# One more product in seven quarter products, with the Z projection's units between them, and moved copies and sums, in a hybrid decoder layer

## The chip, the cores and the metric

One core of a Trainium2 chip runs the whole layer. The metric is device microseconds (us) of one execution. TensorE (PE) multiplies, VectorE (DVE) and ScalarE (ACT) work on the results, the queues of SyncE (SP), ACT and GpSimd (POOL) issue transfers.

## The reference, cut to what matters

The layer has 512 tokens of width 1024. From `h`, the normalised input, it makes three token mixers, merges them under gates and projects the sum. The change touches the third mixer, the gates and the end:

```python
u, v, z = jnp.split(h @ w_in_c, 3, axis=-1)
u = jax.nn.gelu(u)
v = layernorm(jax.nn.gelu(v), ln_g, ln_b)
sp = jnp.einsum('gij,bnjgc->bnigc', wm, vr) + b_s.T[:, :, None]    # vr: v by 128-token chunks
y_c = u * sp.reshape(Bsz, S, MIX_W) * jax.nn.silu(z)
...
g_i = jax.nn.sigmoid(h @ w_in[:, G_OFF + i * D_MODEL:G_OFF + (i + 1) * D_MODEL])
merged = sum over i of g_i * (ys[i] @ w_br[i])
out = rmsnorm(merged @ w_out, g_post)
return x + gate[:, None] * out
```

The v projection, the z and u projections and each gate are products of 512 x 1024 by 1024 x 1024; all are float32.

## The kernel before, in words

**How a product is done.** A float32 operand is split in two fp32r parts, a rounded one (`split`, L71, ACT) and the rest (L72, DVE). Three of the four cross products are taken, so one 128 x 128 x 512 step is three matmuls: L102, L104, L106 in `chan` (channels on the output partitions) and L856, L858, L860 in `passes` (tokens on the output partitions). A pass of 12 matmuls makes 128 tokens by 512 columns over half of the 1024 inputs.

**The chain.** From about 507 us on, everything is a list of units run by `Chain.run`. A unit has a loader, which issues its transfers and gives the steps that split its weights, and a generator, which yields after each matmul. While unit n multiplies, the split steps of unit n+1 are put after its matmuls 1, 2, 3 and so on, extra steps (`also`) at places that L817 sets from the unit's length n, and evictions wait in `later` for a number of matmuls (LAG is 5). These places set only the order of the instructions in each engine's stream. PE, DVE, ACT, SP and POOL each run their stream in that order, and start an instruction as soon as its operands and buffers allow.

**Order of the units.** Gate 0 (4 units of 48 matmuls, `plain`), branch 0 (4 of 48, `add_branch`), gate 1 (7 of 24, `Seven`), branch 1 (4 of 48), v (4 of 48, `plain`), then for each of four column groups a z unit and a u unit (48 each), gate 2 (7 of 24, `Seven`), branch 2 (4 of 48), and the output projection: `out_first(0)`, `out_first(4)` (48 each) and `out_second` (96).

**Seven.** This class makes a product from seven quarter products in place of eight. `p1`, `p2`, `p5`, `p6`, `p7`, `p3`, `p4` run in this order, 24 matmuls each. `p6` adds to the bank that `p1` left in PSUM, `p7` and `p4` add on to the same bank, so a copy of its state (`us`, L927, ACT) must be taken before `p7` writes it. Sums and differences of weight quarters are built in the three tiles `big`: by ACT with factor -1 and a transfer of POOL's queue that accumulates (`minus`, L967 and L968), by such a transfer alone (`plus`, L972), or on DVE (L986). `load` (L962) brings two quarters in, during `p7` and `p3` of the Seven before it (`after`). Results are put together by DVE (`add`, L908) and handed to the evict function. The sums of h that the class needs (`h_sums`) are made once, during gate 0.

**Buffers.** PSUM holds four banks `g`, two `x` (the Sevens' `p1`, `p6`, `p7`, `p4`) and two `t`. `t` serves the transposes of the merged rows (`turn_m`, L1073, released by a split), the spatial product of u (L1130), `gate_sum`, and in `piece` the throw-away output of the Square (L1301). SBUF has five tiles `th`. Each evicted v or u goes through `gelu`, a Square and a Tanh on ACT with DVE steps between them; v ends in `v_evict` and, after the last, `v_norm`. A z unit (`u_z2`) leaves its silu in a `th` tile that the u unit after it uses up; the u unit's result lies in a tile `yc`.

**The end.** During branch 2 the eight steps of `gate(j)` (L1278, L1280) accumulate one fourth of the output gate from transfers of SP's queue. `gate_sum(j)` (L1285, two matmuls into `t`, then L1287 and L1288 on DVE) finishes it. The four calls stand in `out_first(0)` after its last row block, and in `out_first(4)` after the first three. Between these two units ACT's queue issues the loads of x (L1360). `piece(t, e)` takes a finished half of 128 output rows: Square on ACT (L1301), product with the gate on DVE (L1302), and for the second half the root, the sum with x (L1309) and the store.

Of the kernel before, what the change touches and what calls it, by code (L numbers as in the profile page):

```python
# [15 lines left out]
S = 512  # L16
D = 1024
# [20 lines left out]
def hybrid_block(ctx, tc, x, c, g_pre, g_post, w_ada, b_ada, w_in, conv_w, conv_b, pos_ck, w_ck1, w_ck2,  # L38
# [729 lines left out]
    class Chain:  # L768
# [37 lines left out]
        def run(self, upto=None):  # L806
            while self.n < (len(self.units) if upto is None else upto):
                if self.ready is None:
                    self.prepare()
                (w, steps), (_, gen, n, also) = self.ready, self.units[self.n]  # L810
                for f in steps[self.given:]:
                    f()
                self.n += 1
                self.ready, self.given = None, 0
                self.prepare()
                todo = [(1 + k, f) for k, f in enumerate(self.ready[1] if self.ready else [])]
                todo += [(6 + (n - 8) * k // max(1, len(also)), f) for k, f in enumerate(also)]  # L817
                todo.sort(key=lambda x: x[0])
                at = 0
                for _ in gen(w):  # L820
                    at += 1
                    while todo and todo[0][0] <= at:
                        todo.pop(0)[1]()
                    self.tick()
                for _, f in todo:
                    f()
                self.given = len(self.ready[1]) if self.ready else 0
# [64 lines left out]
    class Seven:  # L892


        def __init__(self, src, evict):
            self.src = src
            self.evict = evict
            n = len(mats)
            self.a, self.b, self.c = [big[i] for i in ((0, 1, 2) if n % 2 == 0 else (1, 0, 2))]
            self.after = None  # L900
            if mats:
                mats[-1].after = self
            mats.append(self)
            self.loaded = [False, False]
            ps, us, ys, zs, bs5 = {}, {}, {}, {}, {}

            def add(lag, d, b, t, e):
                chain2.later((lag, lambda: tt(d, b, d, op=OP.add)), (lag + 8, lambda: evict(d, t, e)))  # L908

            def p1(w):  # L910
                for i in range(2):
                    ps[i] = bank("x")
                    yield from passes(ps[i], A11(i), w, True, True)
                    zs[i] = th_tile()
                    chain2.later((LAG, lambda i=i: act(zs[i], ps[i], AF.Copy)))

            def p2(w):
                for i in range(2):
                    z = bank()
                    yield from passes(z, A12(i), w, True, True)  # L920
                    add(18, zs[i], z, i, 0)

            def p6(w):
                for i in range(2):
                    yield from passes(ps[i], S2(i), w, False, True)
                    us[i] = th_tile()
                    chain2.later((LAG, lambda i=i: act(us[i], ps[i], AF.Copy)))  # L927

            def p5(w):
                for i in range(2):  # L930
                    bs5[i] = bank()
                    yield from passes(bs5[i], S1(i), w, True, True)
                    ys[i] = th_tile()
                    chain2.later((LAG, lambda i=i: act(ys[i], bs5[i], AF.Copy)))

            def p3(w):
                for i in range(2):
                    yield from passes(bs5[i], S4(i), w, False, True)
                    add(LAG, us[i], bs5[i], i, 1)

            def p7(w):
                for i in range(2):
                    yield from passes(ps[i], S3(i), w, False, True)
                    add(LAG, ys[i], ps[i], 2 + i, 1)

            def p4(w):
                for i in range(2):
                    yield from passes(ps[i], A22(i), w, False, True)
                    chain2.later((LAG, lambda i=i: evict(ps[i], 2 + i, 0)))

            for load, gen in ((self.l1, p1), (self.l2, p2), (self.l5, p5), (self.l6, p6), (self.l7, p7), (self.l3, p3),
                              (self.l4, p4)):
                chain2.add(load, gen, 24)

        def at(self, i, j, k=0, n=4):
            return self.src[512 * i + 128 * k:512 * i + 128 * (k + n), 512 * j:512 * j + 512].rearrange("(k p) c -> p k c", p=128)
# [80 lines left out]
    def add_branch(i):  # L1037
        src = w_br[0, i]
        bs = {}

        def merge(t, e):
            d = ths.pop((t, e))
            stt(d, d, 1.0, bs[t], op0=OP.add, op1=OP.mult)  # L1043
            if i == 0:
                merged[t, e] = d
                return
            tt(merged[t, e], merged[t, e], d, op=OP.add)
            if i == 2:
                turns.append((t, e))

        def gen(e, k0):
            def f(w):
                for t in range(NB):
                    if k0 == 0:
                        bs[t] = bank()
                    yield from passes(bs[t], y_side(t, k0), w, k0 == 0, k0 == 4)
                    if k0 == 4:
                        chain2.later((LAG, lambda t=t: merge(t, e)))
                    if len(turns) > 2:
                        turn_m(*turns.pop(0))  # L1060
            return f

        for e in range(2):
            for k0 in (0, 4):
                chain2.add(lambda e=e, k0=k0: block(src, k0, 512 * e), gen(e, k0), 48)
# [2 lines left out]

    def turn_m(t, e):

        t_ = t_tile()
        for k in range(4):
            nc.tensor.transpose(t_[:, k * 128:k * 128 + 128], merged[t, e][:, k * 128:k * 128 + 128], ident)  # L1073
        ks = slice(4 * e, 4 * e + 4)
        split(mt[0][:, ks, t * 128:t * 128 + 128], mt[1][:, ks, t * 128:t * 128 + 128],
              t_.rearrange("p (k c) -> p k c", c=128))


    def gelu(src, last):

        th = th_tile()
        act(th, src, AF.Square, scale=GELU_A ** 0.5)
        chain2.later((3, lambda: stt(th, th, 1.0, src, op0=OP.add, op1=OP.mult)),
                     (6, lambda: act(th, th, AF.Tanh, scale=GELU_S)),
# [20 lines left out]
        for t in range(NB):  # L1105
            ts(vg[:, t, :], vg[:, t, :], mv[:, t, 0:1], lr[:, 1, t:t + 1], op0=OP.subtract, op1=OP.mult)

    zs2 = {}

    def u_z2(w):  # L1110
        for e in range(2):
            ps = bank()
            yield from chan(ps, w, e, hh, hl)
            th = zs2[e] = th_tile()
            chain2.later((LAG, lambda th=th, ps=ps: act(th, ps, AF.Tanh, scale=0.5)),
                         (LAG + 3, lambda th=th, ps=ps: stt(th, th, 1.0, ps, op0=OP.add, op1=OP.mult)))

    def u_u2(j):
        def f(w):
            for e in range(2):  # L1120
                ps = bank()
                yield from chan(ps, w, e, hh, hl)

                def last(th, e=e, ps=ps, z=zs2[e]):
                    stt(th, th, 1.0, ps, op0=OP.add, op1=OP.mult)
                    tt(z, z, th, op=OP.mult)
                    g = 2 * j + e
                    t_ = t_tile()
                    for n in range(NB):
                        mm(t_[:, n * 128:(n + 1) * 128], vg[:, n, g * 128:(g + 1) * 128], wst[:, g, :], start=True, stop=True)  # L1130
                    yc[g] = keep.tile([128, S], F, name=f"qy{g}")
                    chain2.later((6, lambda: stt(yc[g].rearrange("p (n i) -> p n i", n=NB), t_.rearrange("p (n i) -> p n i", n=NB),
                                                 lgh[:, g:g + 1], bi[:, g, None, :].to_broadcast([128, NB, 128]),
                                                 op0=OP.mult, op1=OP.add)),
                                 (7, lambda: tt(yc[g], yc[g], z, op=OP.mult)))
                chain2.later((LAG, lambda ps=ps, last=last: gelu(ps, last)))
        return f

# [16 lines left out]
    def chan_load(col):  # L1155
# [1 line left out]
            w, steps = load_w(w_in, col)  # L1157
            return w, [lambda s=s: split(*s) for s in steps]
        return f

    yc = {}

    def h_side(t, k0):
        return lambda k: tuple(a[:, k0 + k, t * 128:t * 128 + 128] for a in (hh, hl))
# [25 lines left out]
    n1 = len(chain2.units)  # L1190
    add_branch(1)
    n2 = len(chain2.units)
    plain(w_in[:, C_V:C_V + D], v_evict)
    n3 = len(chain2.units)
    for j in range(KT // 2):
        chain2.add(chan_load(C_Z + 256 * j), u_z2, 48)
        chain2.add(chan_load(C_U + 256 * j), u_u2(j), 48)
    gates_of(2)
    n4 = len(chain2.units)
# [45 lines left out]
    w_spatial()  # L1245
    chain2.run(n2 + 3)
    b_spatial()
    chain2.run(n3 + 8)
    chain2.flush()
    cst.close()  # L1250
    yst = ExitStack()
# [46 lines left out]

    def piece(t, e):
        cs = slice(512 * e, 512 * e + 512)  # L1300
        act(t_tile(), bs[t], AF.Square, accum_out=s2[:, t, e:e + 1])  # L1301
        tt(ots[t][:, cs], bs[t], gpb[:, cs], op=OP.mult)  # L1302
        if e == 0:
            ts(s2[:, t, 3:4], s2[:, t, 0:1], 1.0 / D, 16.0 * EPS, op0=OP.mult, op1=OP.add)
# [4 lines left out]
            stt(ots[t][:, cs], ots[t][:, cs], s2[:, t, 4:5], xts[t][:, cs], op0=OP.mult, op1=OP.add)  # L1309
            nc.sync.dma_start(out[t * 128:(t + 1) * 128, cs], ots[t][:, cs])  # L1310

    gates_left = list(range(4))

    def out_first(k0):
        def f(w):
            for t in range(NB):
# [2 lines left out]
                yield from passes(bs[t], m_side(t, k0), w, k0 == 0, k0 == 4)  # L1319
                if turns:  # L1320
                    turn_m(*turns.pop(0))
                elif k0 == 0:
                    gate_sum(gates_left.pop(0))
                if k0 == 4:
                    if gates_left:
                        gate_sum(gates_left.pop(0))
                    chain2.later((LAG, lambda t=t: piece(t, 0)))
        return f

# [63 lines left out]
```

## Time and profile before

| | us |
|---|---|
| three runs | 968.57, 969.81, 970.11; median 969.81 |
| the profiled execution | 971.98 |
| its span, first to last instruction | 970.3 |
| mean granted clock of TensorE, share of full speed | 0.992 |
| PE, DVE, ACT busy | 929.1, 686.7, 473.7 |
| slowest lines of the waits of PE after 480 us | 4.7, 2.6, 1.2 |

Start times in rows are us from the span's start. A PE row's duration covers a pipelined matmul, so successive rows overlap; what a matmul costs the stream is the distance between two starts. A wait in brackets is the idle time before the instruction and what ended it.

### The profile page before, as it was taken

How to read it: one execution, taken by the hardware profiler on the slowest of the kernel's cores; microseconds unless marked ns; L12 is line 12 of the kernel's file. 1: busy time of each engine (PE TensorE's matmuls, PEld its weight loads, DVE VectorE, ACT ScalarE, POOL GpSimd, SP SyncE). 2: the span in 40 equal slices, each digit the busy share in tenths (PEclk: the TensorE clock that was granted, in tenths of full speed). 3: DMA queues.
4: the chain of work that ended last, by engine and by line, in shares of the span. 5: the costliest groups of instructions: out<-in, count | busy, mean ns of one | idle time of the engine just before them, and what ended most of it. 6: DMA issues, size and time to landing. Idle time of an engine off the chain costs nothing.

```text
span 970.3 us, 13192 instructions
## 1 busy us (share of the span) xinstructions
PE 929.1 (96%) x4561; PEld 776.6 (80%) x4561; DVE 686.7 (71%) x1673; ACT 473.7 (49%) x1010; POOL 34.3 (4%) x58
## 2 busy tenths in 40 slices
PE   2999999999999999999999999999999999999986
PEld 1789978878887888888888888788878888787765
DVE  5867488998889889989848435645467555657836
ACT  5546366665556666665534415622333334642411
POOL 2010000000000000000010001200000001100000
PEclk9999999999999999999999999999999999999988
DMA  9937021131211213112242424744333323545622
GB/s 288 321 97 221 1 83 49 45 87 44 82 49 48 83 45 87 45 55 76 68 151 87 131 87 88 173 130 124 105 97 109 87 87 67 107 146 177 192 93 88
DMA packets 87337, 101.93 MB, mean 105 GB/s; under 512 B 6841, under 2 KB 67365, under 8 KB 87269
## 3 DMA queue, kind: packets, MB, share of 16 engines
q1 hardware_dynamic: 80484, 86.22, 29.8%
q0 software_dynamic: 4736, 10.66, 5.2%
q10 hardware_dynamic: 2048, 4.19, 1.2%
q8 instruction: 36, 0.59, 0.3%
q14 instruction: 33, 0.26, 0.1%
HBM read 98.96 MB, written 2.10 MB: 104 GB/s over the span
## 4 chain that ended last, share of the span: by engine, by line
PE 69%; issue 14%; DMA 7%; DVE 5%; ACT 2%; POOL 1%; SPq 1%; DVEq 0%; ACTq 0%; POOLq 0%
PE g L102 11%; PE g L104 11%; PE g L106 11%; PE g L858 5%; PE g L860 5%; PE g L856 5%; PE o L697 4%; PE t L686 4%; PE s L664 3%; DMA wa<-in_w_ada_dram 2%; DMA raw<-in_w_out_dram 2%; PE f L273 2%; DMA big<-in_w_in_dram 1%; PE s L471 1%; DVE wl L72 1%
## 5 line engine op out<-in xcount | busy, mean ns | idle before, releaser
L106 PE MATMUL g<-hh,wl 128*128 128x512 f32 x528 | 211.7, 401 | 0.0
L102 PE MATMUL g<-hh,wh 128*128 128x512 f32 x528 | 211.4, 400 | 0.0
L104 PE MATMUL g<-hl,wh 128*128 128x512 f32 x528 | 211.3, 400 | 0.0
L72 DVE TENSOR_TENSOR wl<-raw,wh 128x512 fp32r<-128x512 f32 x228 | 145.4, 686 | 88.8 <-ACT wh L71 81.1
L71 ACT ACTIVATE wh<-raw 128x512 fp32r<-128x512 f32 x228 | 128.1, 622 | 157.6 <-PE g L860 76.3
L104 PEld LDWEIGHTS g<-hl,wh 128*128 128x128 f32 x528 | 99.4, 188 | 16.8
L102 PEld LDWEIGHTS g<-hh,wh 128*128 128x128 f32 x528 | 99.4, 188 | 16.8
L106 PEld LDWEIGHTS g<-hh,wl 128*128 128x128 f32 x528 | 99.4, 188 | 16.6
L676 ACT ACTIVATE p<-p,mx 128x384 f32<-128x384 f32 (+3 forms) x128 | 71.1, 557 | 39.7 <-DVE mx L674 38.9
L856 PE MATMUL g<-wh,y 128*128 128x512 f32 x192 | 75.2, 392 | 0.4 <-DVE qy L1043 0.4
L860 PE MATMUL g<-wh,y 128*128 128x512 f32 x192 | 74.8, 389 | 0.0
L858 PE MATMUL g<-wl,y 128*128 128x512 f32 x192 | 74.7, 389 | 0.0
L71 ACT ACTIVATE ph<-t 128x512 fp32r<-128x512 f32 (+3 forms) x128 | 55.5, 434 | 38.6 <-PE t L686 37.1
L674 DVE CUSTOM_DVE_ANT_0 p<-s,D 128x384 f32<-128x384 f32 (+3 forms) x128 | 60.5, 484 | 18.1 <-PE s L664 17.4
L856 PE MATMUL g<-wh,hh 128*128 128x512 f32 x176 | 71.2, 405 | 0.0
L858 PE MATMUL g<-wl,hh 128*128 128x512 f32 x176 | 69.5, 395 | 0.0
L860 PE MATMUL g<-wh,hl 128*128 128x512 f32 x176 | 69.5, 395 | 0.0
L72 DVE TENSOR_TENSOR pl<-t,ph 128x512 fp32r<-128x512 f32 (+3 forms) x128 | 61.9, 485 | 5.5 <-ACT ph L71 4.4
L686 PE MATMUL t<-ident,p 128*128 128x128 f32 x320 | 56.9, 276 | 1.4 <-DVE pl L72 1.4
L679 DVE TENSOR_SCALAR p<-p,mx,gates 128x384 f32<-128x384 f32 (+3 forms) x128 | 55.5, 442 | 1.7
L72 DVE TENSOR_TENSOR wl<-big,wh 128x1024 fp32r<-128x1024 f32 x24 | 28.7, 1223 | 32.4 <-ACT wh L71 32.4
L664 PE MATMUL s<-kst,qst 128*128 128x288 f32 (+2 forms) x192 | 50.1, 342 | 1.2 <-DVE mx L674 1.2
(296 smaller groups left out, 1646.6 us busy)
## 6 DMA issues: line engine op xcount, KB each, us to landing
raw<-in_w_in_dram SPq DMA_DIRECT2D x180, 256.0 KB, 3.4
raw<-in_w_br_dram SPq DMA_DIRECT2D x48, 256.0 KB, 3.4
big<-in_w_in_dram POOLq DMA_DIRECT2D x20, 512.0 KB, 6.1
wa<-in_w_ada_dram SPq DMA_DIRECT2D x32, 256.0 KB, 6.3
rawg<-in_w_ada_dram SPq DMA_DIRECT2D x16, 256.0 KB, 3.7
raw<-in_w_out_dram SPq DMA_DIRECT2D x16, 256.0 KB, 3.5
rawf<-in_w_in_dram SPq DMA_DIRECT2D x6, 512.0 KB, 6.6
xt<-in_x_dram SPq DMA_DIRECT2D x4, 512.0 KB, 5.2
```

The lines of the kernel that those rows point to most:

```text
L71: act(dst_h, src, AF.Copy)
L72: tt(dst_l, src, dst_h, op=OP.subtract)
L102: mm(ps, w[0][:, k, cs], rh[:, k, :], start=(k == 0), stop=False)
L104: mm(ps, w[0][:, k, cs], rl[:, k, :], start=False, stop=False)
L106: mm(ps, w[1][:, k, cs], rh[:, k, :], start=False, stop=(k == KT - 1))
L664: mm(s_[:, :o + n], q[:, i * 128:(i + 1) * 128], ks[:, z, b, 32 - o:32 + n], start=(z == 0), stop=(z == 1))
L674: nc.vector.tensor_tensor_reduce(out=p, in0=s_, in1=D0[:, S - n:], scale=-slopes[h], scalar=LIM, op0=OP.add, op1=OP.min, accum_out=mx[:, 0 ...
L676: act(p, p, AF.Exp, bias=mx[:, 0, i:i + 1], scale=-1.0, accum_out=mx[:, 1, i:i + 1])
L686: nc.tensor.transpose(t_[:, (i - j) * 128:(i - j + 1) * 128], ps[i][:, j * 128:(j + 1) * 128], ident)
L856: mm(ps, h_, part(w[0], k), start=f, stop=False, skip_group_check=True)
L858: mm(ps, h_, part(w[1], k), start=False, stop=False, skip_group_check=True)
L860: mm(ps, l_, part(w[0], k), start=False, stop=e, skip_group_check=True)
```

## The change

- v becomes a `Seven`. The four z units are put between its products: one after `p2`, one after `p6`, one after `p3`, one after `p4`. The u units then follow one another.
- z is kept in the tile `yc` of its group from the z unit on; the spatial result goes through a `th` tile and is multiplied into it. `gelu` gets three tiles of its own.
- In all three Sevens, `us` is copied at once after its pass in place of 5 matmuls later, and `ys` 9 matmuls later in place of 5.
- The extra steps of a unit (`also`) start a third into it and not at matmul 6. This moves the splits of branch outputs, the sums of h and the steps of `gate`.
- `gate_sum(0)`, `(1)`, `(2)` move to branch 2, after the third row block of its second, third and fourth unit; `gate_sum(3)` takes the place that `gate_sum(0)` had.
- Every second `turn_m` uses a bank `x` in place of `t`; the Square of `piece` writes to a `th` tile in place of `t`.

```diff
-                todo += [(6 + (n - 8) * k // max(1, len(also)), f) for k, f in enumerate(also)]
+                todo += [(n // 3 + (2 * n // 3 - 4) * k // max(1, len(also)), f) for k, f in enumerate(also)]
...
-                    chain2.later((LAG, lambda i=i: act(us[i], ps[i], AF.Copy)))
+                    act(us[i], ps[i], AF.Copy)
...
-                    chain2.later((LAG, lambda i=i: act(ys[i], bs5[i], AF.Copy)))
+                    chain2.later((9, lambda i=i: act(ys[i], bs5[i], AF.Copy)))
...
+            for n, (load, gen) in enumerate(((self.l1, p1), (self.l2, p2), (self.l5, p5), (self.l6, p6), (self.l7, p7),
+                                             (self.l3, p3), (self.l4, p4))):
                 chain2.add(load, gen, 24)
+                for u in between.get(n, ()):
+                    chain2.add(*u)
...
                     if len(turns) > 2:
                         turn_m(*turns.pop(0))
+                    if i == 2 and t == 2 and (e or k0):
+                        gate_sum(2 * e + k0 // 4 - 1)
...
-        t_ = t_tile()
+        t_ = bank("x") if (t + e) % 2 else t_tile()
...
-        th = th_tile()
+        th = cp_.tile([128, S], F, name="ge", bufs=3)
...
-    plain(w_in[:, C_V:C_V + D], v_evict)
+    zu = [(chan_load(C_Z + 256 * j), u_z2(j), 48) for j in range(KT // 2)]
+    Seven(w_in[:, C_V:C_V + D], v_evict, {1: zu[:1], 3: zu[1:2], 5: zu[2:3], 6: zu[3:]})
     n3 = len(chain2.units)
     for j in range(KT // 2):
-        chain2.add(chan_load(C_Z + 256 * j), u_z2, 48)
         chain2.add(chan_load(C_U + 256 * j), u_u2(j), 48)
...
-        act(t_tile(), bs[t], AF.Square, accum_out=s2[:, t, e:e + 1])
+        act(th_tile(), bs[t], AF.Square, accum_out=s2[:, t, e:e + 1])
...
                 if turns:
                     turn_m(*turns.pop(0))
-                elif k0 == 0:
-                    gate_sum(gates_left.pop(0))
+                if k0 == 0 and t == 3:
+                    gate_sum(3)
                 if k0 == 4:
-                    if gates_left:
-                        gate_sum(gates_left.pop(0))
                     chain2.later((LAG, lambda t=t: piece(t, 0)))
```

## Rows read from the trace of the kernel before

**Rows 1.** The page: busy time, share and instructions of each engine.
```profile
PE 929.1 (96%) x4561; PEld 776.6 (80%) x4561; DVE 686.7 (71%) x1673; ACT 473.7 (49%) x1010; POOL 34.3 (4%) x58
```

**Rows 2.** Waits of PE, 480 to 972 us: total, times, longest (us).
```profile
PE t L1285 <- ACT t L1301: 4.7, 1, 4.7
PE x L856 <- ACT th L927: 2.6, 2, 1.9
PE t L1073 <- DVE hl L72: 1.2, 1, 1.2
```

**Rows 3.** PE's timeline in gate 1: start, us, engine, line, operation [idle before].
```profile
599.67 0.39 PE L860 MATMUL g<-wh,hl 128*128 128x512 f32 x1
...
615.31 0.39 PE L860 MATMUL x<-wh,hs1l 128*128 128x512 f32 x1
616.38 0.50 PE L856 MATMUL x<-wh,hs2h 128*128 128x512 f32 x1 [0.68 <-ACT th L927]
```

**Rows 4.** PE's timeline in gate 2, from p6 to p7.
```profile
838.44 0.39 PE L860 MATMUL x<-wh,hs1l 128*128 128x512 f32 x1
840.73 0.50 PE L856 MATMUL x<-wh,hs2h 128*128 128x512 f32 x1 [1.90 <-ACT th L927]
...
844.94 0.39 PE L860 MATMUL x<-wh,hs2l 128*128 128x512 f32 x1
```

**Rows 5.** Windows of 10 us: busy time PE, PEld, DVE, ACT, POOL, PEclk, DMA share, GB/s.
```profile
840.00:850.00 10.00, 9.27 (x34) 7.48 (x35) 6.05 (x8) 5.98 (x10) 0.00 (x0) 0.83 0.18 34
```

**Rows 6.** ACT's timeline in gate 2, same stretch.
```profile
837.09 1.06 ACT L71 ACTIVATE wh<-big 128x1024 fp32r<-128x1024 f32 x1 [0.67 <-DMA big<-in_w_in_dram]
...
839.05 1.14 ACT L71 ACTIVATE y<-qy 128x512 fp32r<-128x512 f32 x2
840.09 0.58 ACT L927 ACTIVATE th<-x 128x512 f32<-128x512 f32 x1
```

**Rows 7.** PE's timeline, output projection.
```profile
916.47 0.66 PE L1073 MATMUL t<-ident,ya 128*128 128x128 f32 x4
...
919.98 0.58 PE L856 MATMUL g<-wh,hh 128*128 128x512 f32 x1
...
925.85 0.39 PE L860 MATMUL g<-wh,hl 128*128 128x512 f32 x1
930.92 1.22 PE L1285 MATMUL t<-acc,ones 128*128 128x256 f32 x2 [4.69 <-ACT t L1301]
...
940.21 0.39 PE L856 MATMUL g<-y,hh 128*128 128x512 f32 x1
```

**Rows 8.** ACT's timeline and its queue (ACTq), output projection.
```profile
918.44 1.56 ACTq L1360 DMA_DIRECT2D big<-in_x_dram  x3
...
927.71 0.63 ACT L71 ACTIVATE y<-raw 128x512 fp32r<-128x512 f32 x1 [1.31 <-DMA raw<-in_w_out_dram]
929.64 0.63 ACT L71 ACTIVATE y<-raw 128x512 fp32r<-128x512 f32 x1 [1.29 <-DMA raw<-in_w_out_dram]
930.17 0.58 ACT L1301 ACTIVATE t<-g 128x512 f32<-128x512 f32 x1
```

**Rows 9.** DVE's timeline, end of branch 2 and output projection.
```profile
915.11 0.69 DVE L1047 TENSOR_TENSOR ya<-ya,qy 128x512 f32<-128x512 f32 x1
...
930.91 0.42 DVE L1287 TENSOR_TENSOR gpb<-t,gpb 128x256 f32<-128x256 f32 x1
```

**Rows 10.** Windows from the start of v to the last u (columns as rows 5).
```profile
676.40:816.80 140.40, 140.40 (x653) 116.77 (x652) 83.90 (x145) 51.59 (x89) 3.96 (x3) 1.00 0.35 97
```

**Rows 11.** Groups by line and shape, 480 to 975 us: busy us, mean ns, idle before.
```profile
L72 DVE TENSOR_TENSOR wl<-raw,wh 128x512 fp32r<-128x512 f32 x132 | 83.7, 687 | 77.0 <-ACT wh L71 76.6
L72 DVE TENSOR_TENSOR wl<-big,wh 128x1024 fp32r<-128x1024 f32 x24 | 28.7, 1223 | 32.4 <-ACT wh L71 32.4
L908 DVE TENSOR_TENSOR th<-g,th 128x512 f32<-128x512 f32 x8 | 5.4, 684 | 0.0
```

**Rows 12.** The page: DMA issues, KB each, median us from issue to landing.
```profile
big<-in_w_in_dram POOLq DMA_DIRECT2D x20, 512.0 KB, 6.1
```

More of the change, by code (lines that the diff above doesn't have):

```diff
@@ L892, in hybrid_block, with __init__ @@
     class Seven:
-        def __init__(self, src, evict):
+        def __init__(self, src, evict, between={}):
             self.src = src
@@ L949, in p4 @@
                     chain2.later((LAG, lambda i=i: evict(ps[i], 2 + i, 0)))
-            for load, gen in ((self.l1, p1), (self.l2, p2), (self.l5, p5), (self.l6, p6), (self.l7, p7), (self.l3, p3),
-                              (self.l4, p4)):
+            for n, (load, gen) in enumerate(((self.l1, p1), (self.l2, p2), (self.l5, p5), (self.l6, p6), (self.l7, p7),
+                                             (self.l3, p3), (self.l4, p4))):
                 chain2.add(load, gen, 24)
+                for u in between.get(n, ()):
+                    chain2.add(*u)
         def at(self, i, j, k=0, n=4):
@@ L1106, in v_norm, with u_z2, f @@
             ts(vg[:, t, :], vg[:, t, :], mv[:, t, 0:1], lr[:, 1, t:t + 1], op0=OP.subtract, op1=OP.mult)
[L1108 to L1116, printed above, removed]
+    yc = {}
+    def u_z2(j):
+        def f(w):
+            for e in range(2):
+                ps = bank()
+                yield from chan(ps, w, e, hh, hl)
+                z = yc[2 * j + e] = keep.tile([128, S], F, name=f"qy{2 * j + e}")
+                chain2.later((LAG, lambda z=z, ps=ps: act(z, ps, AF.Tanh, scale=0.5)),
+                             (LAG + 3, lambda z=z, ps=ps: stt(z, z, 1.0, ps, op0=OP.add, op1=OP.mult)))
+        return f
     def u_u2(j):
@@ L1122, in f, with last @@
                 yield from chan(ps, w, e, hh, hl)
-                def last(th, e=e, ps=ps, z=zs2[e]):
+                def last(th, ps=ps, g=2 * j + e):
+                    z = yc[g]
                     stt(th, th, 1.0, ps, op0=OP.add, op1=OP.mult)
                     tt(z, z, th, op=OP.mult)
-                    g = 2 * j + e
                     t_ = t_tile()
@@ L1130, in last @@
                         mm(t_[:, n * 128:(n + 1) * 128], vg[:, n, g * 128:(g + 1) * 128], wst[:, g, :], start=True, stop=True)
-                    yc[g] = keep.tile([128, S], F, name=f"qy{g}")
-                    chain2.later((6, lambda: stt(yc[g].rearrange("p (n i) -> p n i", n=NB), t_.rearrange("p (n i) -> p n i", n=NB),
+                    d = th_tile()
+                    chain2.later((6, lambda: stt(d.rearrange("p (n i) -> p n i", n=NB), t_.rearrange("p (n i) -> p n i", n=NB),
                                                  lgh[:, g:g + 1], bi[:, g, None, :].to_broadcast([128, NB, 128]),
                                                  op0=OP.mult, op1=OP.add)),
-                                 (7, lambda: tt(yc[g], yc[g], z, op=OP.mult)))
+                                 (7, lambda: tt(z, z, d, op=OP.mult)))
                 chain2.later((LAG, lambda ps=ps, last=last: gelu(ps, last)))
@@ L1159, in chan_load @@
         return f
-    yc = {}
     def h_side(t, k0):
@@ L1247, in hybrid_block @@
     b_spatial()
-    chain2.run(n3 + 8)
+    chain2.run(n3 + 4)
     chain2.flush()
@@ L1310, in piece @@
             nc.sync.dma_start(out[t * 128:(t + 1) * 128, cs], ots[t][:, cs])
-    gates_left = list(range(4))
     def out_first(k0):
```

## The prediction

> **What bounds the kernel now.** I read the page's busy times first: PE is busy for 96% of the span, DVE for 71% [rows 1]. Next the waits of PE after 480 us, where all that changes lies: three lines, 8.5 us together, are nearly all it waits [rows 2]. So time can be won in two ways only, with fewer matmuls or with these waits. Then PE's timeline, for what one matmul costs. From 599.67 to 615.31 us, 69 starts follow each other without a wait: 15.64 / 69 = 0.2267 us each [rows 3]. The 0.39 us in each row is the length of a pipelined matmul and not its price.
>
> The waits cost more than their own length. Before `p7` of gate 1 the distance is 1.07 us in place of 0.23, so about 0.9 us are lost with the slower start behind it [rows 3]. Before `p7` of gate 2 it is 2.29 us, and from there to 844.94 us twelve matmuls take 6.50 us in place of 12 x 0.2267 = 2.72: 3.8 us lost, since the matmuls behind the wait run slower [rows 4]. The granted clock of that window is 0.83 [rows 5], so a part of it was at 1.2 GHz and not at 2.4. Both waits end with the copy of `us`. In gate 2, ACT is late because a weight split waits for an accumulated transfer until 837.09 us, and two splits of y stand between it and the copy, which starts at 840.09 [rows 6].
>
> The largest loss is in `out_first(4)`. It begins at 919.98 us; 48 matmuls at 0.2267 are 10.9 us, but `out_second` begins at 940.21, 20.2 us later [rows 7]. The wait of 4.7 us is that of the third `gate_sum`: its bank `t` is held by the Square of `piece`, which ACT starts at 930.17 only, since before it four weight splits wait for w_out blocks, and these land late behind the loads of x that ACT's queue issued from 918.44 on [rows 8].
>
> **The change, part by part.**
>
> *Fewer matmuls.* v takes 4 x 48 = 192 now, 7 x 24 = 168 after. 24 x 0.2267 = **-5.4 us** [rows 3], with all else on PE kept (the spatial and bias products stay). The Trainium skill, TensorE: Matmul & The Clock Gate, section "Wait — 56ns, not 53.3ns?", gives 215.7 ns for back-to-back matmuls of 512 columns; by that the term would be 5.2 us. The trace's 0.2267 differs, and the trace is used.
>
> *What the seven products add on ACT and DVE.* On DVE: 12 splits of 128x1024 and 2 differences at 1.22, 4 splits and 6 sums at 0.69, less 16 splits at 0.69 [rows 11]: 17.1 + 6.9 - 11.0 = +13 us. From v's start to u's end DVE is busy for 83.9 of 140.4 us [rows 10]; 97 of 135 stays under PE, so it hides on the mean. Locally it is tight: while the first z unit runs, DVE has two splits, two differences, two sums and two gelu chains, then the bias steps, and the splits for `p6` come last. I follow that order at the rows' durations and get the first of these split 0.4 us after PE could want it. Neither wait is in the trace; the near rows are the two `p7` waits, 0.9 and 3.8 us [rows 3, 4]. I take **+0.5** (bounds 0 and +3.8). The copy of `us` has a z unit behind it in v, 48 x 0.2267 = 10.9 us, so the `p7` wait doesn't appear there. An accumulating transfer takes 6.1 us to land [rows 12], and in v a z unit lies between most issues and uses. Their POOL queue holds little else than the mask of w_s, which is done before the first is wanted.
>
> *Copies of `us` and `ys`.* In gate 1 the order on ACT is the same: split, transfer wait, evict, `ys`, `us`. The wait stays: 0. In gate 2, one of the two y splits now comes after the copy, not both before it: half of 1.14 us [rows 6], **-0.5 us** against a stall that costs 3.8. I leave the clock's fall in, since 1.90 - 0.5 = 1.4 us [rows 4] lies between 0.68 in gate 1 [rows 3], without a fall, and 1.90, with one; bounds: -4.7, with both waits gone, and 0.
>
> *Sums, splits and gate steps moved.* A place in a unit is only an order. In gate 0 no DVE instruction of the unit changes its order with respect to these steps, and ACT's evictions keep theirs near enough: 0, covered by what DVE has done before PE wants it (branch 0 starts more than a unit later); without that cover one split, 0.69. In branch 2 the steps of `gate` fall behind the merges they stood before; SP issues the same transfers in the same order, so its queue is unchanged.
>
> *`gate_sum` moved, banks changed.* The 1.2 us wait of the transpose on `t` [rows 2] goes, as its bank is now an `x` that was free. But three `gate_sum`s bring PE their matmuls there, and DVE two steps of 0.42 [rows 9] each, and DVE is the engine that is late at this place: its last merge ends at 915.80 [rows 9], and PE transposes that tile at 916.47 [rows 7]. So what PE wins before, it waits for there. I take the start of that transpose 0.7 us later (one `gate_sum` of 0.85 that isn't hidden, less a little of order); bounds -1.3, the wait gone, and +2.5, three times 0.85.
>
> *The end.* `out_first(4)` has no `gate_sum` left, so nothing on PE asks for `t`; it ends at 919.98 + 10.9 = 930.9. What is late next is the bank of `out_second`'s first block, freed by the Square and the gate product of the first piece. ACT still waits for w_out: last split at 929.64 + 0.6, Square to 930.8; on DVE the split and the gate product, 0.69 each, end at 931.7. With the 0.7 from branch 2: 932.4 against 940.21, **-7.8 us**, branch 2 included. Bounds: -9.5, if PE alone sets it and branch 2 loses nothing; -4.0, if the w_out blocks come two distances (2 x 1.93 us [rows 8]) later. From there to the end nothing changes.
>
> **Sum:** -5.4 + 0.5 - 0.5 - 7.8 = -13.2 us. The profiled execution took 971.98, 1.7 over its span; it would become 958.8. It lies 2.2 above the median of the three runs, 969.81, so I give 969.81 - 13.2 = **956.6**.
>
> **Rivals.**
>
> *The transfers hold the end.* The loads of x and the last w_out blocks share the engines, and PE arrives earlier. The blocks landed 1.93 us apart [rows 8]; two such distances more give 956.6 + 3.9 = 960.5. For it: this stretch is bound by them already. Against: the loads of x start by ACT's place in the stream, hardly moved, and the bytes are the same.
>
> *DVE holds v.* Around `p3` DVE has 4 + 2 splits, two sums and two gelu chains in 2 x 5.4 us; if the second-next z unit gets the bank that a sum of `p3` still has to read, PE stops there as before `p7` of gate 2, 3.8 us [rows 4]: 956.6 + 3.8 = 960.4. Whether it does depends on which of the four `g` banks is free first; two others are free by then. In the trace the third `gate_sum` started with the end of a Square, at 930.92, as the second's bank was only being read at 930.91 [rows 7 to 9]: so it had taken another bank than that one, and banks don't just go around in turn.
>
> *Gate 2 is healed.* With the wait short enough, the clock stays: -2.2 more; with gate 1's 0.9 also gone, 956.6 - 3.1 = 953.5. For it: the wait in gate 1 was not followed by slow matmuls. Against: the transfer of gate 2 lands no sooner.
>
> *Slower: the accumulated weights come late.* Five of v's products (`p5`, `p6`, `p7`, `p3`, `p4`) use quarters that POOL's queue brings or corrects. If each landed so late that PE stopped as in gate 2, 5 x 3.8 = 19 us: 956.6 + 19 = 975.6. It decides where landing exceeds what lies between issue and use, some 16 us with a z unit, against 6.1 on the median [rows 12]. In gate 2, where no z unit stands between, ACT's wait for one was 0.67 [rows 6]. The Trainium skill, SBUF — State Buffer, section "SBUF: two separate sides", speaks for this rival: GpSimd can't write the descriptors of its transfers while DVE runs an instruction in a two-port mode, so that the transfer seems to stand still. The trace of before does not show such a lock, as none of the rows here has a transfer of that queue late beside a busy DVE.
>
> *It does not do what it says,* all is given back: PE would then have 24 matmuls fewer and as much more waiting, 969.8.
>
> **How the numbers follow.** Chances: forecast 0.53, transfers at the end 0.13, DVE in v 0.15, gate 2 healed 0.14, weights late 0.03, given back 0.02. The range from 952.0 to 962.5 holds the first four cases with 1.5 to 2 us of the bounds on either side. A measurement of this kernel can tell 0.2%, 1.9 us, from no change. All cases but two lie beyond that on the fast side: faster 0.95, same 0.02, slower 0.03.
>
> **What would show it.** The page of after should have 24 PE instructions fewer. The waits of PE should have no L1285 line of 4.7 us, the `us` line with 2.0 to 2.2 us, and none above 1 us between the start of v and the end of u. `out_second` should begin some 12 us after `out_first(4)`, not 20. I am wrong if v's stretch has a wait of 2 us or more, or a granted clock below 1.00; if `out_second` starts 16 us after; or if DVE's merges stop PE in branch 2 by more than 2.5 us.

## The result and the profile after

The changed kernel took 959.65 us (median of 4 runs, 958.56 to 959.88) beside 969.76 for the kernel before (4 runs): a ratio of 0.9896, 95% interval 0.9879 to 0.9913. Timed once more later it took 957.83 beside 969.20: 0.9886, interval 0.9863 to 0.9910. The change is worth 10.1 us by the first measurement and 11.4 by the second. The forecast was 956.6, with a range from 952.0 to 962.5.

Of the profile after, first the page's busy times, in the columns of [rows 1]:

```profile
PE 920.5 (96%) x4537; PEld 771.0 (80%) x4537; DVE 698.9 (73%) x1681; ACT 486.7 (51%) x1020; POOL 44.1 (5%) x68
```

PE has 24 instructions fewer, DVE is busy 12.2 us longer (the step for DVE said 13; within v, z and u it is 96.91 against 83.90). The waits of PE from 480 us on answer to [rows 2]:

```profile
PE x L856 <- ACT th L927: 4.1, 2, 3.2
PE g L856 <- DVE s L1308: 1.1, 1, 1.1
PE t L1077 <- DVE ya L1049: 0.2, 1, 0.2
```

The 4.7 us of the third `gate_sum` (L1285 before) are gone. The wait for the `us` copy has grown from 2.6 to 4.1, and a new one of 1.1 stands in its place at the end. None of them lies in v, z or u. The window from the start of v to the end of u, as [rows 10]:

```profile
677.60:812.60 135.00, 135.00 (x630) 112.30 (x628) 96.91 (x155) 63.14 (x99) 11.30 (x11) 1.00 0.47 119
```

PE is busy in all of it at a granted clock of 1.00, and it is 135.0 us long and not 140.4. Gate 2 on the timelines of POOL, ACT and PE, as [rows 4, 6]; one fence for each engine:

```profile
825.79 1.19 POOL L970 DMA_DIRECT2D big<-in_w_in_dram  x1 [0.25 <-ACT big L969]
```
```profile
834.74 1.06 ACT L71 ACTIVATE wh<-big 128x1024 fp32r<-128x1024 f32 x1 [2.60 <-DMA big<-in_w_in_dram]
...
837.22 0.59 ACT L927 ACTIVATE th<-x 128x512 f32<-128x512 f32 x1
```
```profile
837.85 0.50 PE L856 MATMUL x<-wh,hs2h 128*128 128x512 f32 x1 [3.25 <-ACT th L927]
```

ACT now waits 2.60 us for the accumulated transfer, where it waited 0.67 [rows 6]. From its split to the copy of `us` are 837.22 - 834.74 = 2.48 us, where they were 840.09 - 837.09 = 3.00: one y split less stands between. So the moved copy does what it should, and the transfer, which lands 8.95 us after its issue, takes more than that away.

The end, as [rows 7] on PE, [rows 8] on ACT and its queue, [rows 9] on DVE:

```profile
914.79 0.58 PE L856 MATMUL g<-wh,hh 128*128 128x512 f32 x1
...
927.15 0.50 PE L856 MATMUL g<-y,hh 128*128 128x512 f32 x1 [1.11 <-DVE s L1308]
```
```profile
913.80 1.44 ACTq L1360 DMA_DIRECT2D big<-in_x_dram  x3
915.55 0.63 ACT L71 ACTIVATE y<-raw 128x512 fp32r<-128x512 f32 x1 [1.29 <-DMA raw<-in_w_out_dram]
919.34 0.63 ACT L71 ACTIVATE y<-raw 128x512 fp32r<-128x512 f32 x1 [3.16 <-DMA raw<-in_w_out_dram]
923.22 0.63 ACT L71 ACTIVATE y<-raw 128x512 fp32r<-128x512 f32 x1 [3.24 <-DMA raw<-in_w_out_dram]
925.13 0.63 ACT L71 ACTIVATE y<-raw 128x512 fp32r<-128x512 f32 x1 [1.29 <-DMA raw<-in_w_out_dram]
925.67 0.58 ACT L1305 ACTIVATE th<-g 128x512 f32<-128x512 f32 x1
```
```profile
925.80 0.69 DVE L72 TENSOR_TENSOR y<-raw,y 128x512 fp32r<-128x512 f32 x1 [1.23 <-ACT y L71]
926.41 0.68 DVE L1306 TENSOR_TENSOR ot<-g,gpb 128x512 f32<-128x512 f32 x1
927.01 0.14 DVE L1308 TENSOR_SCALAR s<-s 128x1 f32<-128x1 f32 x1
```

`out_second` starts 12.4 us after `out_first(4)` and not 20.2. What is late now is the bank of the first piece: PE waits for DVE's product (L1306 and the small L1308 behind it), DVE for ACT's last split of w_out, and ACT for the blocks behind the loads of x: its last four splits of them start 3.8, 3.9 and 1.9 us apart.

**Stage by stage.** Each column is the distance between the first matmuls of two units on PE's timeline; the last runs to the end of the span. There are two profiled executions of the kernel before and three of the changed kernel; the repeats are the experiments `before_again`, `after_again` and `after3`. What differs between rows of one kernel belongs to the execution.

| us | chain starts at | to v | v to gate 2 `p2` | gate 2, `p6` to `p3` | branch 2 | `out_first(0)` to `out_second` | to the end |
|---|---|---|---|---|---|---|---|
| before | 506.74 | 169.63 | 145.98 | 14.68 | 48.10 | 33.32 | 30.09 |
| before_again | 506.59 | 169.75 | 145.97 | 12.95 | 47.47 | 31.92 | 30.09 |
| changed | 507.76 | 169.83 | 140.53 | 14.44 | 47.29 | 25.54 | 30.85 |
| after_again | 506.49 | 170.05 | 140.53 | 15.68 | 47.13 | 24.91 | 30.85 |
| after3 | 508.54 | 169.88 | 140.53 | 14.09 | 47.32 | 27.39 | 30.89 |
| mean, changed less before | +0.9 | +0.2 | -5.4 | +0.9 | -0.5 | -6.7 | +0.8 |

The two pieces between, `p2` and `p5`, `p3` and `p4`, take 10.88 us in all five. From v on, the last row adds to -10.9 us, and with gate 1's 0.2 to -10.7.

### The profile page after: what moved, and what is told of

Its sections match the earlier page's. It is cut to its first block, busy times and chain, and to the rows that moved or that the text cites. A ratio compares the mean times of both kernels' runs of the same rounds, so it can differ in the third digit from the quotient of the medians.

```text
span 958.0 us, 13143 instructions
## 1 busy us (share of the span) xinstructions
PE 920.5 (96%) x4537; PEld 771.0 (80%) x4537; DVE 698.9 (73%) x1681; ACT 486.7 (51%) x1020; POOL 44.1 (5%) x68
## 4 chain that ended last, share of the span: by engine, by line
PE 69%; issue 14%; DMA 7%; DVE 6%; ACT 2%; POOL 1%; SPq 1%; DVEq 0%; ACTq 0%; POOLq 0%
PE g L102 11%; PE g L104 11%; PE g L106 11%; PE g L856 4%; PE g L858 4%; PE g L860 4%; PE o L697 4%; PE t L686 4%; PE s L664 3%; DMA wa<-in_w_ada_dram 2%; DMA big<-in_w_in_dram 2%; PE x L856 2%; PE f L273 2%; PE x L858 2%; PE x L860 2%
## 5 line engine op out<-in xcount | busy, mean ns | idle before, releaser
L71 ACT ACTIVATE wh<-raw 128x512 fp32r<-128x512 f32 x216 | 122.0, 622 | 127.9 <-PE g L860 54.3
L72 DVE TENSOR_TENSOR wl<-raw,wh 128x512 fp32r<-128x512 f32 x216 | 137.8, 686 | 60.5 <-ACT wh L71 52.6
L72 DVE TENSOR_TENSOR wl<-big,wh 128x1024 fp32r<-128x1024 f32 x36 | 42.8, 1222 | 49.5 <-ACT wh L71 49.5
L71 ACT ACTIVATE wh<-big 128x1024 fp32r<-128x1024 f32 x36 | 36.6, 1053 | 38.4 <-PE g L860 17.4
L856 PE MATMUL g<-wh,hh 128*128 128x512 f32 x120 | 47.3, 394 | 0.0
L860 PE MATMUL g<-wh,hl 128*128 128x512 f32 x120 | 46.8, 390 | 0.0
```

The source lines that it names most:

```text
L71: act(dst_h, src, AF.Copy)
L72: tt(dst_l, src, dst_h, op=OP.subtract)
L856: mm(ps, h_, part(w[0], k), start=f, stop=False, skip_group_check=True)
L860: mm(ps, l_, part(w[0], k), start=False, stop=e, skip_group_check=True)
```

## The experiments

Times are medians, each beside the kernel before timed together with it.

**Parts alone, on the kernel before.** `tail_only` has the moved `gate_sum`s and the changed banks, nothing else:

```diff
+                    if i == 2 and t == 2 and (e or k0):
+                        gate_sum(2 * e + k0 // 4 - 1)
...
-        t_ = t_tile()
+        t_ = bank("x") if (t + e) % 2 else t_tile()
...
-        act(t_tile(), bs[t], AF.Square, accum_out=s2[:, t, e:e + 1])
+        act(th_tile(), bs[t], AF.Square, accum_out=s2[:, t, e:e + 1])
...
```

> The kernel before with the end's part alone: gate_sum in branch 2, every second transpose on a bank x, the Square of piece into a th tile. If the parts add as predicted: 7.8 us less than before, out_second some 12 us after out_first(4). Rival, that the profiled execution of before had a fall of the clock which the timed ones mostly lack (it lies 2.2 us above their median): the end is worth 6 us or less in the times, though its profile shows 12 us between the two units as well.

Measured: 964.38 beside 969.36, ratio 0.9938 (0.9919 to 0.9957), -5.0 us. The L1285 wait is gone from its profile; `out_second` waits 0.9 for DVE's small step behind the product (here L1306), as in the whole change. From 640 us on, so without gate 1, PE has two waits left:

```profile
PE x L856 <- ACT th L927: 2.0, 1, 2.0
PE g L856 <- DVE s L1306: 0.9, 1, 0.9
```

Its stage from `out_first(0)` to `out_second` is 25.24, against 33.32 and 31.92: 6.7 to 8.1 us won there. The time shows less, as the rival said (6 us or less). The profiled execution lost some of its gain elsewhere: gate 2 had slow matmuls (14.78), and the chain began at 508.03. And the first profiled execution of before was 2.2 us slower than the median run. How much of each lies in the medians is not shown.

`seven_only` has v as a Seven with the z units between, and `gelu`'s own tiles, with all other edits undone:

```diff
-    plain(w_in[:, C_V:C_V + D], v_evict)
+    zu = [(chan_load(C_Z + 256 * j), u_z2(j), 48) for j in range(KT // 2)]
+    Seven(w_in[:, C_V:C_V + D], v_evict, {1: zu[:1], 3: zu[1:2], 5: zu[2:3], 6: zu[3:]})
...
```

> The kernel before with v in seven quarter products and the z units between them, and nothing else moved. By the count of matmuls: 5.4 us less than before, no wait of PE between the start of v and the end of u, and the old end (20 us between out_first(4) and out_second). Rival, DVE holds v: a wait of PE of 1 us or more in v, and 3 us less or fewer.

Measured: 964.11, ratio 0.9943 (0.9927 to 0.9959), -5.25 us; v to gate 2 takes 140.53, exactly as in the whole change, and PE has no wait there (from 640 us on):

```profile
PE t L1287 <- ACT t L1303: 3.6, 1, 3.6
PE x L856 <- ACT th L927: 1.8, 1, 1.8
PE t L1075 <- DVE hl L72: 0.3, 1, 0.3
```

`copies_only` moves the copies of `us` and `ys` in the kernel before:

```diff
-                    chain2.later((LAG, lambda i=i: act(us[i], ps[i], AF.Copy)))
+                    act(us[i], ps[i], AF.Copy)
...
-                    chain2.later((LAG, lambda i=i: act(ys[i], bs5[i], AF.Copy)))
+                    chain2.later((9, lambda i=i: act(ys[i], bs5[i], AF.Copy)))
```

> The kernel before with the copies of us at once and of ys 9 matmuls later, nothing else. By the order on ACT: 0.5 us less in gate 2, nothing in gate 1, so 0 to 0.5 us in the time. Rival, the copy was late because of its place and not because of the transfer: both waits before p7 go, 3 to 4.7 us less. If the length of the wait before p7 follows the landing of the accumulated transfer, it varies from run to run by 1 us or more at the same code.

Measured: 968.26, ratio 0.9986 (0.9973 to 0.9998), -1.1 us; the interval holds the 0.5 expected and rules out the rival's 3 to 4.7. On ACT the copy starts 2.48 us after the split that waits for the transfer, 3.00 before the edit:

```profile
838.74 1.06 ACT L71 ACTIVATE wh<-big 128x1024 fp32r<-128x1024 f32 x1 [0.87 <-DMA big<-in_w_in_dram]
...
841.22 0.59 ACT L927 ACTIVATE th<-x 128x512 f32<-128x512 f32 x1
```

The three parts add to -5.0 - 5.25 - 1.1 = -11.3 us; the whole was -10.1 and -11.4. All three were timed together, on another chip than the second measurement of the whole. They don't work against each other by more than the runs can tell.

**The places of L817.** `no_also` is the changed kernel with the old places:

```diff
-                todo += [(n // 3 + (2 * n // 3 - 4) * k // max(1, len(also)), f) for k, f in enumerate(also)]
+                todo += [(6 + (n - 8) * k // max(1, len(also)), f) for k, f in enumerate(also)]
```

> The changed kernel with the extra steps of a unit back at matmul 6 and on (L817 undone); the rest as changed. If a place is only an order: the time of the changed kernel, 959.7, within 0.5 us. Rival: the steps of gate stand before the merges again, the merges come later by three of them (1.5 us), PE waits for them in branch 2, and the time is 1 to 2 us longer.

Measured: 956.67, ratio 0.9868 (0.9852 to 0.9884). That is 3.0 us below the 959.65 of the changed kernel, whose interval it hardly touches, but the two were not timed together. Neither the expectation (the same time) nor its rival (slower) had said so. Its profile differed from that of the changed kernel in two stages: gate 2 (12.60 against 14.44), where the transfer landed 7.13 us after its issue and not 8.95, and `out_first(0)` to `out_second` (24.55 against 25.54). Five runs decided what that was worth. `old24` and `old48` undo L817 for one length of unit each (here `old24`; `old48` has `n >= 48` in place of `n < 48`):

```diff
+                todo += [(6 + (n - 8) * k // max(1, len(also)) if n < 48 else n // 3 + (2 * n // 3 - 4) * k // max(1, len(also)), f) for k, f in enumerate(also)]
```

> The changed kernel with line 817's old places for the side work of the 24-matmul units alone (the y splits and the sums of h in the chain's first products and of both gates); the gate steps of branch 2 and the last w_out splits stay at the new places. Theory A (gate 2's 1.8 us and the end's 0.9 us are two separate losses, each from the steps of its own stage): this one gets gate 2's back, 959.6 - 1.8 = 957.8, gap before gate 2's seventh product near 1.8 instead of 3.63, gap before out_second still near 1.5. Theory B (the late landing of the seventh product's last weight half, 8.95 us after its issue, is chance of one profiled execution, and all of the loss lies in the end and branch 2): 959.6, no change.

> The changed kernel with line 817's old places for the side work of the 48-matmul units alone (branch 2's gate steps, the last w_out splits); the y splits and sums stay at the new places. Theory A: gets the end's 0.9 us and some 0.3 between back, 959.6 - 1.2 = 958.4, gap before out_second near 0.6. Theory B: gets all 3.0 us back, 956.7.

> The changed kernel once more, unedited, for a second profiled execution. Theory A: the seventh product's last weight half of gate 2 lands again near 8.95 us after its issue, and TensorE waits 3.25 to 3.7 us for ScalarE's splits there. Theory B: it lands near 7.1 us after its issue, as in the five other profiles, and the wait is near 1.5 us.

Measured together, the kernel before at 970.44: `old24` 959.29, ratio 0.9880 (0.9858 to 0.9902); `old48` 959.95, 0.9882 (0.9862 to 0.9902); `after_again`, a single run, 959.10. Neither half shows the 3 us, though the intervals leave room for 2; the transfer landed late in all three (8.99, 8.63 and 8.54 us after issue). `old24` doesn't get gate 2's loss back, as theory A asked of it. Then the changed kernel and the one with the old places were timed side by side:

> The changed kernel unedited, timed again, so that the next kernel stands beside it on one chip. Theory A (the new places of line 817 cost about 3 us): 2 to 3 us above the kernel with the old places timed in the same call. Theory B (the 3.0 us lay between two measurements on different chips: the last weight half of gate 2's seventh product landed 7.1 us after its issue in the profiles taken in one call and 8.4 to 8.95 us in those of the other): within 1 us of it, and both show the same landing.

> The changed kernel with line 817's old places, timed beside the unedited one. Theory A: 2 to 3 us faster than it, landing near 7.1 us in gate 2. Theory B: within 1 us of it, and the landing is that of the unedited kernel in the same call.

Measured: `after3` 957.83, ratio 0.9886 (0.9863 to 0.9910); `no_also2` 958.16, ratio 0.9884 (0.9861 to 0.9906). Theory B: the places cost nothing that these runs can tell, and the 3.0 us were the distance between two measurements. The two profiles of the same code, `no_also` and `no_also2`, taken on two different chips, show one piece of such a distance. POOL and ACT of the first:

```profile
824.83 1.19 POOL L970 DMA_DIRECT2D big<-in_w_in_dram  x1 [0.25 <-ACT big L969]
```
```profile
830.18 1.05 ACT L71 ACTIVATE wh<-big 128x1024 fp32r<-128x1024 f32 x1
831.96 1.06 ACT L71 ACTIVATE wh<-big 128x1024 fp32r<-128x1024 f32 x1 [0.73 <-DMA big<-in_w_in_dram]
```

and of the second:

```profile
824.94 1.19 POOL L970 DMA_DIRECT2D big<-in_w_in_dram  x1 [0.25 <-ACT big L969]
```
```profile
830.29 1.05 ACT L71 ACTIVATE wh<-big 128x1024 fp32r<-128x1024 f32 x1
833.65 1.06 ACT L71 ACTIVATE wh<-big 128x1024 fp32r<-128x1024 f32 x1 [2.31 <-DMA big<-in_w_in_dram]
```

From the start of v to 830.2 us every row of the second stands 0.09 to 0.14 later. Then the same transfer lands 1.6 us later in it; the part on the copies, below, says what held it up.

**The kernel before once more.**

> The kernel before, unedited, for a second profiled execution. If TensorE's clock falls behind the wait at gate 2's seventh product whenever there is one, the wide spacing of the matmuls (0.43 us instead of 0.23) is there again for some 12 of them; if the fall is by chance of one execution, the wait stands near 2 us without it and the span is shorter by some 2 us. Landing of gate 2's last accumulated weight half: near 7.1 us if it is the schedule's, near 8.5 to 8.9 us if it goes with the chip of the call.

Measured: 968.17 us, 3.8 less than the first profiled execution. Its window from `p7` of gate 2 on, against [rows 5], the first matmul of `p7`, against [rows 4], and its waits of PE from 480 us on, against [rows 2]:

```profile
840.00:850.00 10.00, 9.43 (x42) 7.81 (x42) 7.32 (x9) 6.98 (x11) 0.00 (x0) 1.00 0.17 30
```
```profile
840.57 0.50 PE L856 MATMUL x<-wh,hs2h 128*128 128x512 f32 x1 [1.77 <-ACT th L927]
```
```profile
PE t L1285 <- ACT t L1301: 4.5, 1, 4.5
PE x L856 <- ACT th L927: 2.6, 2, 1.8
PE t L1073 <- DVE hl L72: 0.5, 1, 0.5
PE t L1073 <- DVE ya L1047: 0.4, 1, 0.4
```

Nearly the same wait, 1.77 us and not 1.90, but 42 matmuls in the window in place of 34, at a granted clock of 1.00 in place of 0.83. The stage is 1.73 us shorter. With 0.63 in branch 2 and 1.40 in the output projection that is the whole difference.

The 1.40 is the clock again. `out_first(4)`, from its first matmul to that of `out_second`, in `before`, `before_again` and `after`, in the columns of [rows 5]:

```profile
919.98:940.21 20.23, 15.54 (x56) 12.32 (x55) 8.09 (x19) 4.50 (x10) 0.00 (x0) 0.83 0.38 137
```
```profile
917.60:936.41 18.81, 14.30 (x56) 11.42 (x55) 8.06 (x19) 4.50 (x10) 0.00 (x0) 0.91 0.40 147
```
```profile
914.79:927.15 12.36, 11.25 (x51) 9.00 (x49) 4.82 (x11) 3.91 (x9) 0.00 (x0) 1.00 0.66 241
```

PE waits 4.7 and 4.5 us there in the first two, and 1.1 us at the end of the third. The clock lost 0.17 of 20.23 us in the first, an estimated 3.4 us, half as much in the second and nothing in the changed kernel. So of the 9.3 us that the prediction read as the loss of `out_first(4)`, about 3.4 were a fall of the clock, which goes with the wait.

The landing in gate 2 is 6.95 us, on the chip on which `after3`, `no_also2` and `x_old` have 8.59 to 8.71: the late one does not go with the chip alone.

**Two attempts at the waits that are left.** `p3_old` is `no_also` with `p3` ahead of `p7` (the edit against `no_also`, as for `x_old` below):

```diff
-            for n, (load, gen) in enumerate(((self.l1, p1), (self.l2, p2), (self.l5, p5), (self.l6, p6), (self.l7, p7),
-                                             (self.l3, p3), (self.l4, p4))):
+            for n, (load, gen) in enumerate(((self.l1, p1), (self.l2, p2), (self.l5, p5), (self.l6, p6), (self.l3, p3),
+                                             (self.l7, p7), (self.l4, p4))):
```

> The changed kernel with all of line 817's old places and Seven's third product put ahead of its seventh, at both gates and in the spatial values: the accumulated weights of the seventh product and the copies it reads get 24 more matmuls (24 x 0.227 = 5.4 us). If TensorE's only stops in a gate are for those two, the gap before the seventh product goes: 1.8 us of gate 2 and 1.0 of gate 1, 956.7 - 2.5 = 954.2, with no clock fall there. Rival: the third product's own weights (a plain load) then come late, or the copies' banks come free later, and the stop moves to another product: 956.5 to 957.5.

Measured: 959.46 beside 970.44, ratio 0.9876 (0.9855 to 0.9898). The stop moved to another product, as the rival said, though not for its reasons (late weights of `p3`, or the banks of the copies). The wait for the copy of `us` is gone, and PE stops before `p4`:

```profile
849.54 0.47 PE L856 MATMUL x<-wh,hh 128*128 128x512 f32 x1 [2.06 <-DVE th L908]
...
853.22 0.50 PE L856 MATMUL x<-wh,hh 128*128 128x512 f32 x1 [0.72 <-DVE th L908]
```

`p4` adds on to the banks that `p7` has just written, and must let DVE read them first; `p3` between the two was what gave DVE that time. In gate 1 the two new waits are 1.64 and 0.68, where the old one was 0.7 to 1.1.

`x_old` is `no_also` with the loads of x issued one output unit later:

```diff
-    chain2.run(n5 + 1)
+    chain2.run(n5 + 2)
     for t in range(NB):
         nc.scalar.dma_start(xts[t], x[t * 128:(t + 1) * 128, :])
```

> The changed kernel with line 817's old places and the x loads issued one output unit later, so that ScalarE's queue goes to the last w_out splits about 1.3 us (four issues) earlier. If out_second's start waits on those splits (through VectorE behind them), its wait goes: 0.6 to 1.1 us less than the kernel with the old places alone. Rival: the x rows then land after the first pieces ask for them, and the end is no earlier or later: 0 to +2 us.

Measured: 958.64, ratio 0.9887 (0.9862 to 0.9912). On ACT's timeline the splits come earlier, as thought:

```profile
917.26 0.63 ACT L71 ACTIVATE y<-raw 128x512 fp32r<-128x512 f32 x1 [0.68 <-DMA raw<-in_w_out_dram]
919.79 1.27 ACT L71 ACTIVATE y<-raw 128x512 fp32r<-128x512 f32 x2 [1.90 <-DMA raw<-in_w_out_dram]
920.97 0.58 ACT L1305 ACTIVATE th<-g 128x512 f32<-128x512 f32 x1
```

The last splits begin at 919.79 and the first Square at 920.97, 4.7 us earlier than in the changed kernel, and `out_second` waits for nothing. But its stage from `out_first(0)` to `out_second` is 24.17, against 24.55 in both profiles of `no_also`: 0.4 us won in the profile, and nothing in the time. PE was only just late there.

No version was shown to beat the changed kernel: the ratios of `old24`, `old48`, `p3_old` and `x_old` lie within the interval of its second measurement, and that of `no_also` came back to the changed kernel's when the two were timed side by side.

## Why the prediction was right, and where it was not

**Fewer matmuls, -5.4.** v to gate 2 is 5.44 us shorter in every profile with the seven products, that of `seven_only` among them. 24 x 0.2267 = 5.44.

**Stalls in v, +0.5.** None came. PE has no wait in the window above, although DVE is busy for 96.9 of 135 us. Both rivals that put a wait there fall: DVE holding v, and the accumulated weights being late. Ten of POOL's big transfers lie in that window, and a z unit stood between issue and use as the step said of most.

**Copies of `us` and `ys`, -0.5: this is the step that failed.** Its own working came true, 3.00 us from split to copy became 2.48, in `copies_only` and in the whole change. But it took the landing of the transfer as given. The step's bound on the bad side was 0, and gate 2 became 0.9 us longer on the mean; the wait for `us` was to be 2.0 to 2.2 us in both gates together and is 4.1. Counted from the second issue (L968, after the change L970) to the split that waited for it, the landing was 6.95 to 7.27 us in both profiles of before and those of `tail_only`, `copies_only` and `seven_only`. Of the eight profiles of the changed kernel and its variants with `p7` in its old place, seven have 8.54 to 8.99 us and one, `no_also`, 7.13. (The 6.1 us that the prediction took from [rows 12] is a median over all of POOL's loads, plain ones among them.)

What came in between can be read in the traces. They record sixteen updates of the transfer's semaphore, one for each part of it. In the changed kernel fifteen come 6.5 to 7.0 us after the issue, about as in before, and the last at 8.93. DMA queue q8, which the page calls `instruction`, moves a block of 16 KB every 24 to 36 us from 500 us on. The DMA queues of the changed kernel from 832 to 834 us, and of before in the same stretch of the transfer, from 836 to 838:

```profile
q0 software_dynamic: 195, 0.37, 106.5%
q8 instruction: 1, 0.02, 2.9%
```
```profile
q0 software_dynamic: 206, 0.39, 110.4%
```

In the changed kernel the block starts 6.88 us after the issue and takes 0.94 us, just when the transfer's parts end; in before it starts 3.0 us ahead of the issue. This sorts the profiles: in all eight late ones (the seven and `p3_old`) the block starts 6.5 to 6.9 us after the issue, and the one late part comes 1.05 to 1.20 us after the block's end. In the four with the old v it starts 2.4 to 3.0 us ahead of the issue, and the landing is early. So with v as a Seven a block falls into this transfer, which the step did not count. In `no_also` and `seven_only` it falls there too, at 6.6 and 6.4 us, and no part is late; both were taken on one chip, on which no late profile is on record, and why these two escaped stays open, as does why the others' one part waited. No run moved a block alone, so this is read off the traces and not tested by an edit.

A rival is that POOL was held up. The Trainium skill, SBUF — State Buffer, section "SBUF: two separate sides", says that GpSimd cannot write a transfer's descriptors while DVE runs an instruction in a two-port mode. No run here shows that to be the difference: from 820 to 830 us `no_also` and `no_also2` have DVE's and POOL's busy times within 0.2 us of each other in every window of 2 us.

**"Gate 2 healed", 953.5, and the clock.** I expected the granted clock to stay at full speed if the wait got short enough. The length of the wait does not decide it: see the last section. The fall costs 1.6 us, less than the rival's 2.2, for which [rows 4] give 6.50 - 2.72 for the loss less 2.06 for the wait, 1.7: the 24 matmuls of `p7` take 7.2 us in the profiles with it and 5.6 in those without.

**Sums, splits and gate steps moved, 0.** It stands: 957.83 and 958.16 side by side. The intervals leave room for 2 us either way.

**The end, -7.8 with branch 2.** Branch 2 and the stage to `out_second` give -0.8 - 7.8 between the first two profiles, and -0.5 - 6.7 = -7.2 between the means: the first execution of before was the worse of the two by 2.0 us here. What is late next was named rightly, the last w_out block, ACT's Square and DVE's product, in this order. The step itself had `out_second` wait for them, 0.8 us by its own sum; the waits in the three profiles are 1.1, 0.4 and 1.2. The rival's 3.9 us more did not come, though two of the blocks now lie 3.9 us apart. (The bound with PE alone is 9.3 by [rows 7], 940.21 - 930.9, and not 9.5.) The waits for the merged rows (L1049), put at 0.7, are 0.2, 0.4 and 1.7. The step did not name the clock: about 3.4 of the 9.3 us lost in `out_first(4)` were a fall that went with the wait, and `before_again` had half of it, so part of the -7.8 was the first execution's own. What the step called unchanged was not quite: from `out_second` to the end it is 0.8 longer. Nearly all of it, 0.6, lies behind DVE's last instruction, where the last store runs; `seven_only` has it (30.70), `tail_only` has not (30.19). I did not trace it further.

**The sum.** -13.2 was forecast, -10.7 measured by stages: gate 2 is 1.4 us worse than its term, the end of the kernel 0.8, the output stage 0.6, gate 1 0.2, and v 0.5 better: -13.2 + 1.4 + 0.8 + 0.6 + 0.2 - 0.5 = -10.7. The forecast also took terms read from one execution, 971.98 us, off a median 2.2 below it. Part of what they took away, the slow output stage, was that execution's own.

## What to carry to other kernels

Profile the same kernel twice before reading a wait of 1 to 2 us as its property: here two executions of one program differed by 1.7 us in a clock fall, 1.6 us in one transfer's landing (on two chips) and up to 2.5 us in the output stage. Compare two variants only side by side on one chip; a difference of 3 us between two measurements, with intervals that hardly touched, vanished when both ran so. When one transfer lands late with nothing changed around it, look in its stretch for a block on the `instruction` queue. And before a unit is moved to cover a wait, ask what it covered where it stood: `p3` gave DVE the time to read the banks that `p4` adds to.

## What I had not expected of the hardware

TensorE's granted clock fell to half behind the wait at `p7` of gate 2 in four of the thirteen profiles that have this wait, and how long PE had waited does not sort them: it fell after 1.90, 2.02, 2.85 and 3.02 us, and stayed after nine others of 1.43 to 3.29, among them 1.77, 2.90, 3.25 and 3.29. Two executions of the changed kernel, the same window of each, in the columns of [rows 5]; first `after_again`, which had waited 2.85 us:

```profile
834.00:848.00 14.00, 11.60 (x44) 9.39 (x45) 9.52 (x11) 9.34 (x15) 0.00 (x0) 0.88 0.20 36
```

and `after3`, which had waited 2.90:

```profile
834.00:848.00 14.00, 11.10 (x50) 8.84 (x48) 9.44 (x12) 10.05 (x15) 0.00 (x0) 1.00 0.34 61
```

The first has the lower granted clock and six matmuls fewer, though it is busy for longer. PE's timeline of `after_again` shows the fall itself:

```profile
837.67 0.55 PE L860 MATMUL x<-wh,hs2l 128*128 128x512 f32 x1
838.01 0.63 PE L856 MATMUL x<-wh,hs2h 128*128 128x512 f32 x1
838.44 0.63 PE L858 MATMUL x<-wl,hs2h 128*128 128x512 f32 x1
```

The distance of two starts goes from 0.23 to 0.43 us, about that of 2.4 and 1.2 GHz, after five matmuls at full speed, and comes back to 0.23 some eight matmuls later.

The granted clock also goes with the time of a whole run. Among the 37 runs of the kernel before that were timed beside these experiments, those with a mean of 0.990 took 972.8 to 973.7 us, those with 0.995 took 968.3 to 969.9, and the one with 0.998 took 965.7.
